# The first loads in smaller parts in order of need, two projections in halves of the channels, and the last scaling in four equal parts

## The chip, the cores and the metric

The kernel runs on one core of one Trainium2 chip. TensorE (PE) multiplies matrices into PSUM, VectorE (DVE) and ScalarE (ACT) do elementwise work, GpSimd (POOL) a little of it, and the queue of SyncE (SP) issues all transfers between the chip's memory and the on-chip buffers. The metric is the device time of one execution in microseconds (us); lower is better. The instructions of an engine stand in one order in the program, and one that waits holds up those behind it on that engine.

## The reference

Two residual layers on 1024 positions of 1024 channels; each is a token mixer and a feed-forward block, with an RMS norm ahead of each and one at the end. What bears on this change is the very beginning, the norm and input projection of layer 0, and the very end, the final norm:

```python
def rms_norm(x, g):
    y = xf * lax.rsqrt(jnp.mean(xf * xf, axis=-1, keepdims=True) + EPS)
    return y * g

def mixer_ab(h, w_in, conv_w, a_log, dt_bias, norm_g, sc_conv_w, w_out):
    qkv, z, beta_raw, alpha_raw, gate_b, gate_c, sc_in = split_cols(h @ w_in, AB_SPLITS)
    qkv = jax.nn.silu(causal_depthwise_conv(qkv, conv_w))
    ...

    h = x
    for layer in range(DEPTH):
        hn = rms_norm(h, norm_mix_g[layer])
        ...
    return rms_norm(h, norm_final_g)
```

## The kernel before

Everything is kept transposed, channels on the 128 partitions: x is 8 tiles of 128 channels (index `d` or `k`) for each of two halves of the sequence (`half`, 512 positions). A float32 product is made of three matmuls on split operands: a value is split into a rounded high part and a rest, and `mm3` issues high x high (L125), high x low (L126) and low x high (L127). `split` (L99 to L102) makes the parts: a CAST on ACT for the high one, then a subtraction on DVE for the rest. A projection (`proj`, L133) is 8 channel tiles x 3 = 24 matmuls of 128x512 into one PSUM bank. Banks come from three rings: "u" with three (`psu`), "m" with three (`psm`), "g" with two (`psg`).

The norm of layer 0 is put off. `scaled_in` (L1878) multiplies a tile of x by the gain `g` alone: ACT makes `hnh`, DVE the rest `hnl`. The projections run on these, and the factor 1/rms, one per position, is multiplied in afterwards. It is made by `squares` and `piece` (ACT squares a tile into `sq`, of which there are two buffers; DVE adds it to `acc`, L186), by `rms` (16 tiny matmuls on `acc` and `sq`, L198; here called the sums; then `v` on DVE, L201, and a power on POOL, L203), and by `spread` (four transposes, L212), after which ACT copies the result to `rb[half]` (L866). `lead` (L849) then multiplies a finished projection by `rb` on DVE into `xp`, which frees its PSUM bank.

At the start one queue issues the loads in the order of the program: the vector of gains `vec`, x tile 0, weight block 0 (128x1024, `raw`), x tiles 1 to 3, the second weight block, x tiles 4 to 7, and so on. Both `raw` buffers are in use by then, so blocks three and four wait until the splits of the first two are done. A weight block holds 8 slices of 128 columns, one for each channel tile.

While `ordered` is open (L1915 to its `close()`), the instructions of PE, DVE and ACT stand in the order in which the code names them; work from behind it (the convolution's `cacc`, L1023 and L1025, and the one-off `na`, L930) may be set between by the scheduler where its cost rules see room. In that stretch PE does, for half 0: two projections, the sums, half of a third projection, the spread, its other half, a fourth projection; then for half 1 one projection, the sums of half 1 (L198 again), a second projection, its spread. The step function `second` (L1885) puts the operands and squares of half 1 between these on ACT and DVE. Behind that come 32 matmuls on the small block `wba` (L902), whose results DVE scales into `bat` (L905) and PE transposes with L907.

At the very end, `last` in `down` computes the last output tile in two halves of 256 positions. For each, `scaled` (L1951) multiplies all 8 channel tiles by the spread 1/rms on DVE and writes them out; three DVE instructions of 4, 2 and 2 channel tiles, each with its own transfer.

Of the kernel before, what the change touches and what calls it, by code (L numbers as in the profile page):

```python
# [18 lines left out]
P = 128  # L19
T_LEN = 1024  # L20
DM = 1024
KT = DM // P
NH = 2
HT = 512
# [4 lines left out]
KH = KT // 2  # L29
# [21 lines left out]
W_AT = weight_chunks()  # L51
# [3 lines left out]
def hybrid_trunk_kernel(ctx: ExitStack, tc: tile.TileContext, x_t, w_all, w_down, w_ba, vecs, c_f, c_i, c_rope, out):  # L55
    nc = tc.nc
    V, S, G, T = nc.vector, nc.scalar, nc.gpsimd, nc.tensor
    dma = nc.sync.dma_start

    def pool(name, side="left", space=None):  # L60
        kw = {} if space is None else {"space": space}
        if space is None:
            kw["side"] = side
        if space is not DRAM:
            kw["reuse_waits"] = "tile"
        return tc.tile_pool(name=name, bufs=1, **kw)
# [22 lines left out]
    def psg():  # L89
        return ps.tile([P, HT], F32, tag="g", name="psg", bufs=2)  # L90
# [8 lines left out]
    def split(hi, lo, src, eng=V):  # L99

        S.copy(hi, src)  # L101
        eng.tensor_tensor(lo, src, hi.bitcast(F32), op=SUB)  # L102
# [15 lines left out]
    def wk(w, i):  # L118

        return tuple(w[i][:, z, :].rearrange("p (k c) -> p k c", k=KT) for z in range(2))  # L120
# [12 lines left out]
    def proj(w, hn, order=range(KT), o=None, first=True, last=True):  # L133
        o = psu() if o is None else o
        mm3(o, [(w[0][:, k, :], w[1][:, k, :], hk(hn, 0, k), hk(hn, 1, k)) for k in order], first, last)
        return o
# [693 lines left out]
    def mixer_ab(hn, rb, hp, tr, first, second, close):  # L830
# [16 lines left out]
        wqk, wvz = first  # L847
# [9 lines left out]
            return xp  # L857

        early = {}
        os3 = [proj(wk(wqk, 0), hn[0]), proj(wk(wqk, 1), hn[0])]  # L860
        r = tr.rms(0)
        os3.append(proj(wk(wvz, 0), hn[0], range(KH), last=False))
        pb = tr.spread(r)
        proj(wk(wvz, 0), hn[0], range(KH, KT), os3[2], first=False)
        second(0)
        S.copy(rb[0], pb)  # L866
        for which, o in enumerate(os3):
            early[0, which] = lead(o, 0)
        early[0, 3] = proj(wk(wvz, 1), hn[0])
        second(1)  # L870
        early[1, 0] = proj(wk(wqk, 0), hn[1])
        second(2)
# [4 lines left out]
        with ExitStack() as es:  # L877
# [9 lines left out]
            raw = fp.tile([P, KT, 8], F32, name="wba_raw")  # L887
# [982 lines left out]

    mes = ExitStack()
    hp = mes.enter_context(pool("mix"))
    dma(vec, vecs)
    tr.begin(0, x_t[0], (0,))
    hn = [[quarter(), quarter()] for _ in range(NH)]
    rb = [hp.tile([P, HT], F32, name=f"rb{half}") for half in range(NH)]

    def scaled_in(half, d):  # L1878

        x, g = tr.at(half, d), vec[:, R_MIX + d:R_MIX + d + 1]  # L1880
        hi, lo = hk(hn[half], 0, d), hk(hn[half], 1, d)
        S.activation(hi, x, AF.Copy, scale=g)
        V.scalar_tensor_tensor(lo, x, g, hi.bitcast(F32), op0=MULT, op1=SUB)  # L1883
# [10 lines left out]
        else:  # L1894
            S.copy(rb[1], tr.spread(r.pop()))

    def coming(name):

        u, raw = unit(), ring.tile([P, DM], F32, tag="raw", name="raw", bufs=2)
        dma(raw, w_all[W_AT[name]])  # L1900
        return u, raw

    def arrived(u, raw):
        split(u[:, 0, :], u[:, 1, :], raw)
        return u

    def squares(half, ds):
# [3 lines left out]
    E = mybir.EngineType  # L1911
    ordered = ExitStack()
    ordered.enter_context(tc.manual_schedule(engines={E.PE, E.DVE, E.Activation}))
    w0 = coming(("ab", 0))
    tr.load(0, x_t[0], range(1, 4))  # L1915
    w1 = coming(("ab", 4))
    tr.load(0, x_t[0], range(4, KT))
    dma(cf[:, 0:P], c_f[:, 0:P])
    scaled_in(0, 0)
    first = [[arrived(*w0)], []]  # L1920
    for d in range(1, 4):
        scaled_in(0, d)
    first[0].append(arrived(*w1))
    w0, w1 = coming(("ab", 8)), coming(("ab", 12))
    ring.tile([P, 24], F32, name="pad")
    tr.begin(1, x_t[1])
# [23 lines left out]

    def scaled(half, cols, pb):  # L1951

        for a, b in ((0, 4), (4, 6), (6, 8)):
            h = tr.h[half][a // KH][:, a % KH:a % KH + b - a, cols]
            V.tensor_tensor(h, h, pb[:, None, :].to_broadcast([P, b - a, pb.shape[1]]), op=MULT)
            dma(out[half, a:b, :, cols].rearrange("k p t -> p k t"), h)
# [135 lines left out]
```

## Time and profile before

| | |
|---|---|
| Time, median of 3 runs | 2595.95 us (2595.7 to 2596.75) |
| Profiled execution: its own time | 2595.86 us |
| Profiled execution: span of the profile | 2594.1 us |
| PE busy | 2574.8 us, 99% of the span |
| DVE, ACT, POOL busy | 1649.9, 1003.9, 457.7 us (64%, 39%, 18%) |
| First projection matmul starts | 7.38 us into the span |
| Last DVE instruction starts its group of three | 2587.56 us |

The span runs from the first to the last event of the profile; 1.76 us of the execution's own time lie outside it. A row of the timeline gives start, duration, engine, source line, operation, and output<-input; "xN" is N such instructions in a row, merged, so that the gap from one to the next is somewhat less than the duration of a single one. What stands in square brackets is how long the engine sat idle before and what ended that.

### The profile page before, as it was taken

What the parts mean: (1) busy time and instruction counts of PE and PEld (TensorE: products, weight loads), DVE (VectorE), ACT (ScalarE), POOL (GpSimd) and SP (SyncE); (2) the same over time, 40 slices, a digit from 0 to 9 for tenths busy, and PEclk for the clock granted to TensorE, in tenths of its full rate; (3) what the DMA queues carried; (4) which work ended last, traced back from release to release, by engine and by line L of the source; (5) the groups of instructions that cost most, each with busy time, mean ns of one, the idle gap of its engine ahead of it and who ended that gap; (6) DMA issues with size and microseconds to landing.
All of it is one profiled execution on the core that took longest, in us unless ns stands there. A gap on an engine that the chain in (4) does not pass through costs nothing.

```text
span 2594.1 us, 36983 instructions
## 1 busy us (share of the span) xinstructions
PE 2574.8 (99%) x14203; PEld 2153.8 (83%) x14203; DVE 1649.9 (64%) x2784; ACT 1003.9 (39%) x1655; POOL 457.7 (18%) x434
## 2 busy tenths in 40 slices
PE   8999999999999999999999999999999999999998
PEld 6888888888888888888888888888888888888887
DVE  7887776585656565564675557478567565566554
ACT  5432123343333345333454345354444333334442
POOL 1110111333333300010000000000034433331001
PEclk9999999999999999999999999999999999999999
DMA  4434446424555688541222322314652455668853
GB/s 143 139 99 153 122 152 213 153 86 162 189 195 204 205 302 284 190 134 62 82 64 73 92 64 62 99 58 127 221 198 70 171 175 202 203 206 282 285 172 122
DMA packets 239697, 402.95 MB, mean 155 GB/s; under 512 B 30080, under 2 KB 114592, under 8 KB 239392
## 3 DMA queue, kind: packets, MB, share of 16 engines
q1 hardware_dynamic: 239520, 400.59, 46.7%
q8 instruction: 111, 1.82, 0.3%
q14 instruction: 66, 0.54, 0.1%
HBM read 280.36 MB, written 120.14 MB: 154 GB/s over the span
## 4 chain that ended last, share of the span: by engine, by line
PE 80%; DVE 2%; issue 0%; ACT 0%; POOLq 0%; POOL 0%; DVEq 0%; ACTq 0%
PE psu L125 16%; PE psu L127 16%; PE psu L126 16%; PE psg L125 5%; PE psg L127 5%; PE psg L126 5%; PE psm L126 4%; PE psm L127 4%; PE psm L125 4%; PE psm L1724 1%; PE psm L1698 1%; PE psg L1489 1%; PE psm L1713 1%; DVE h L586 1%; PE psm L198 0%
## 5 line engine op out<-in xcount | busy, mean ns | idle before, releaser
L125 PE MATMUL psu<-hnh,w 128*128 128x512 f32 x1328 | 530.5, 399 | 7.4 <-ACT w L101 7.4
L127 PE MATMUL psu<-hnh,w 128*128 128x512 f32 x1328 | 520.0, 392 | 0.0
L126 PE MATMUL psu<-hnl,w 128*128 128x512 f32 x1328 | 519.2, 391 | 0.0
L102 DVE TENSOR_TENSOR w<-raw,w 128x1024 fp32r<-128x1024 f32 (+1 forms) x314 | 374.5, 1194 | 150.5 <-ACT w L101 149.5
L101 ACT CAST w<-raw 128x1024 fp32r<-128x1024 f32 (+1 forms) x314 | 306.0, 976 | 298.8 <-PE psu L127 146.7
L125 PEld LDWEIGHTS psu<-hnh,w 128*128 128x128 f32 x1328 | 250.2, 188 | 57.3 <-ACT w L101 7.4
L127 PEld LDWEIGHTS psu<-hnh,w 128*128 128x128 f32 x1328 | 249.8, 188 | 53.7 <-DVE w L102 0.8
L126 PEld LDWEIGHTS psu<-hnl,w 128*128 128x128 f32 x1328 | 250.4, 189 | 49.5 <-DVE hnl L1883 0.6
L186 POOL TENSOR_TENSOR acc<-acc,sq 128x512 f32<-128x512 f32 x48 | 71.6, 1492 | 496.0 <-ACT sq L182 496.0
L102 DVE TENSOR_TENSOR hidq<-hr,hidq 128x1024 fp32r<-128x1024 f32 x72 | 81.5, 1134 | 72.4 <-ACT hidq L101 72.3
L296 POOL TENSOR_TENSOR ws<-raw 128x512 f32<-128x512 f32 x40 | 54.8, 1371 | 355.0 <-DMA raw<-in_dram 249.9
L125 PE MATMUL psu<-w,hnh 128*128 128x512 f32 (+1 forms) x320 | 113.3, 354 | 0.0
L102 DVE TENSOR_TENSOR w<-ws,w 128x1024 fp32r<-128x1024 f32 x38 | 50.7, 1334 | 97.4 <-ACT w L101 97.3
L127 PE MATMUL psu<-w,hnl 128*128 128x512 f32 (+1 forms) x320 | 111.4, 348 | 0.0
L126 PE MATMUL psu<-w,hnh 128*128 128x512 f32 (+1 forms) x320 | 111.3, 348 | 0.0
L101 ACT CAST hidq<-hr 128x1024 fp32r<-128x1024 f32 x72 | 70.2, 979 | 97.6 <-DMA hr<-ts 56.7
L125 PE MATMUL psm<-hidq,w 128*128 128x512 f32 (+1 forms) x275 | 106.1, 386 | 0.0
L126 PE MATMUL psm<-hidq,w 128*128 128x512 f32 (+1 forms) x275 | 106.0, 385 | 0.0
L127 PE MATMUL psm<-hidq,w 128*128 128x512 f32 (+1 forms) x275 | 106.0, 385 | 0.0
L1527 POOL COPY attn<-ac 32x128 f32<-32x128 f32 x32 | 13.3, 416 | 430.8 <-DVE ac L1493 378.4
L125 PE MATMUL psu<-hidq,w 128*128 128x512 f32 (+1 forms) x220 | 84.7, 385 | 0.0
L126 PE MATMUL psu<-hidq,w 128*128 128x512 f32 (+1 forms) x220 | 84.6, 384 | 0.0
(431 smaller groups left out, 5719.3 us busy)
## 6 DMA issues: line engine op xcount, KB each, us to landing
raw<-in_dram SPq DMA_DIRECT2D x228, 512.0 KB, 3.7
sd<-in_dram SPq DMA_DIRECT2D x44, 512.0 KB, 3.8
hid<-hid SPq DMA_DIRECT2D x88, 256.0 KB, 2.7
sd<-sd SPq DMA_DIRECT2D x44, 512.0 KB, 3.3
hr<-ts SPq DMA_DIRECT2D x40, 512.0 KB, 4.2
raw<-sd SPq DMA_DIRECT2D x40, 512.0 KB, 4.4
hd<-h SPq DMA_DIRECT2D x48, 256.0 KB, 3.9
h<-hd SPq DMA_DIRECT2D x48, 256.0 KB, 5.8
```

Of the source, the lines that this page charges most:

```text
L101: S.copy(hi, src)
L102: eng.tensor_tensor(lo, src, hi.bitcast(F32), op=SUB)
L125: T.matmul(o, lh, rh, start=first and i == 0, stop=False, **kw)
L126: T.matmul(o, lh, rl, start=False, stop=False, **kw)
L127: T.matmul(o, ll, rh, start=False, stop=last and i == n - 1, **kw)
L186: (eng or G).tensor_tensor(a, a, q, op=ADD)
L296: G.tensor_tensor(s[:, HT:], b[:, :HT], b[:, HT:], op=ADD)
L586: eng.tensor_tensor(dst, x, y, op=SUB)
L1489: T.matmul(od[r * 32:(r + 1) * 32, c * 32:(c + 1) * 32], a[:, z], x[:, z], start=True, stop=True, tile_position=(0, r * 32))
L1698: T.matmul(o[:, z], self.q[:, j * P:(j + 1) * P], self.k[:, (j - m + 1) * P:(j + 1) * P], start=True, stop=True)
L1713: T.transpose(o[:, i:i + P], s[:, i:i + P], ident)
L1724: T.matmul(po[:, jj * P:(jj + 1) * P], pt[:, z.start + i * P:z.start + (i + 1) * P], self.vp[:, j - m + 1 + i, :], start=i == 0, stop=i == ...
```

## The change

Four things change. (1) `vec` is loaded behind x tile 0 and not ahead of it. Weight block 0 is loaded and split in two parts, the first 2 of its 8 slices and then the other 6, and block 1 as 4 and 4 slices; x tile 1 is loaded and scaled between the parts of block 0. (2) The first two projections are done in four pieces: channels 0 to 3 of the first, 0 to 3 of the second, 4 to 7 of the first, 4 to 7 of the second. (3) The third projection is done whole ahead of the sums of half 0, and it is the fourth that is split by the spread; the fourth gets a bank of the ring "g", the others stay in "u". (4) `scaled` has four instructions of two channel tiles each, and four transfers.

```diff
         early = {}
-        os3 = [proj(wk(wqk, 0), hn[0]), proj(wk(wqk, 1), hn[0])]
+        os3 = [proj(wk(wqk, i), hn[0], range(KH), last=False) for i in range(2)]
+        for i in range(2):
+            proj(wk(wqk, i), hn[0], range(KH, KT), os3[i], first=False)
+        os3.append(proj(wk(wvz, 0), hn[0]))
         r = tr.rms(0)
-        os3.append(proj(wk(wvz, 0), hn[0], range(KH), last=False))
+        early[0, 3] = proj(wk(wvz, 1), hn[0], range(KH), psg(), last=False)
         pb = tr.spread(r)
-        proj(wk(wvz, 0), hn[0], range(KH, KT), os3[2], first=False)
+        proj(wk(wvz, 1), hn[0], range(KH, KT), early[0, 3], first=False)
         second(0)
         S.copy(rb[0], pb)
         for which, o in enumerate(os3):
             early[0, which] = lead(o, 0)
-        early[0, 3] = proj(wk(wvz, 1), hn[0])
         second(1)
         early[1, 0] = proj(wk(wqk, 0), hn[1])
...
+    tr.begin(0, x_t[0], (0,))
     dma(vec, vecs)
-    tr.begin(0, x_t[0], (0,))
...
-    def coming(name):
+    def coming(name, at=DM):
 
         u, raw = unit(), ring.tile([P, DM], F32, tag="raw", name="raw", bufs=2)
-        dma(raw, w_all[W_AT[name]])
-        return u, raw
-
-    def arrived(u, raw):
-        split(u[:, 0, :], u[:, 1, :], raw)
+        dma(raw[:, :at], w_all[W_AT[name]][:, :at])
+        return u, raw, lambda: dma(raw[:, at:], w_all[W_AT[name]][:, at:])
+
+    def arrived(u, raw, _, a=0, b=DM):
+        split(u[:, 0, a:b], u[:, 1, a:b], raw[:, a:b])
         return u
...
-    w0 = coming(("ab", 0))
-    tr.load(0, x_t[0], range(1, 4))
-    w1 = coming(("ab", 4))
+    w0 = coming(("ab", 0), 2 * P)
+    tr.load(0, x_t[0], (1,))
+    w0[2]()
+    tr.load(0, x_t[0], (2, 3))
+    w1 = coming(("ab", 4), HT)
+    w1[2]()
     tr.load(0, x_t[0], range(4, KT))
     dma(cf[:, 0:P], c_f[:, 0:P])
     scaled_in(0, 0)
-    first = [[arrived(*w0)], []]
-    for d in range(1, 4):
+    arrived(*w0, 0, 2 * P)
+    scaled_in(0, 1)
+    first = [[arrived(*w0, 2 * P, DM)], []]
+    for d in range(2, 4):
         scaled_in(0, d)
-    first[0].append(arrived(*w1))
+    arrived(*w1, 0, HT)
+    first[0].append(arrived(*w1, HT, DM))
...
-        for a, b in ((0, 4), (4, 6), (6, 8)):
+        for a in range(0, KT, 2):
+            b = a + 2
```

The rows below are the program's order on one engine; "xN" stands for N like rows in a row, and in brackets is what an instruction waits for. DMAHW0, DMAHW1 and so on are the transfers of SP's queue counted in turn, so that at the start DMAHW0 is the first and DMAHW1 the second; `hnh` and `hnl` are the parts of scaled x, `w` a weight block's parts, `h_97` and `h_96` the x tiles 0 to 3 of half 0. First ACT at the start of the program, before:

```order
L930 ACT_TABLE_LOAD
L930 ACTIVATE na<-vec 128x4 [waits DMAHW0_49]
L1882 ACTIVATE hnh<-h_97,vec 128x512 [waits DMAHW1_49]
L101 CAST w<-raw 128x1024 [waits DMAHW2_49]
L1882 ACTIVATE hnh<-h_97,vec 128x512 [waits DMAHW3_49]
```

The same place with the change:

```order
L1884 ACT_TABLE_LOAD [waits DMAHW1_49]
L1884 ACTIVATE hnh<-h_96,vec 128x512 [waits DMAHW0_49]
L101 CAST w<-raw 128x256 [waits DMAHW2_49]
L1884 ACTIVATE hnh<-h_96,vec 128x512 [waits DMAHW3_49]
L101 CAST w<-raw 128x768 [waits DMAHW4_49]
L1884 ACTIVATE hnh<-h_96,vec 128x512 [waits DMAHW5_49]
```

The loading of the activation table was free of waits and stood ahead of `na`; now it waits for the second transfer, which is `vec`, and `na` has moved behind the first part of block 1.

The second place is DVE between `v` of half 0 and the last of the six additions to `acc` for half 1, `h_145` and `h_146` (with the change `h_151` and `h_152`) being the x tiles of half 1. Before, from `v` to the fourth of the additions:

```order
L201 TENSOR_SCALAR v_262<-psm 128x4
L1883 SCALAR_TENSOR_TENSOR hnl<-h_145,vec,hnh 128x512 x4
L856 TENSOR_TENSOR xp<-psu,rb_108 128x512 x2
L1023 TENSOR_SCALAR cacc<-xp,vec 128x512 x2
L1025 SCALAR_TENSOR_TENSOR cacc<-xp,vec,cacc 128x512
L856 TENSOR_TENSOR xp<-psu,rb_108 128x512
L1883 SCALAR_TENSOR_TENSOR hnl<-h_146,vec,hnh 128x512 x4
L186 TENSOR_TENSOR acc<-acc,sq 128x512
L102 TENSOR_TENSOR wba<-wba_raw,wba 128x8x8
L186 TENSOR_TENSOR acc<-acc,sq 128x512
L1025 SCALAR_TENSOR_TENSOR cacc<-xp,vec,cacc 128x512
L186 TENSOR_TENSOR acc<-acc,sq 128x512
```

With the change:

```order
L201 TENSOR_SCALAR v_293<-psm 128x4
L1885 SCALAR_TENSOR_TENSOR hnl<-h_151,vec,hnh 128x512 x4
L102 TENSOR_TENSOR wba<-wba_raw,wba 128x8x8
L856 TENSOR_TENSOR xp<-psu,rb_108 128x512 x3
L1885 SCALAR_TENSOR_TENSOR hnl<-h_152,vec,hnh 128x512 x4
L186 TENSOR_TENSOR acc<-acc,sq 128x512
L1025 TENSOR_SCALAR cacc<-xp,vec 128x512
L186 TENSOR_TENSOR acc<-acc,sq 128x512
L1027 SCALAR_TENSOR_TENSOR cacc<-xp,vec,cacc 128x512
L186 TENSOR_TENSOR acc<-acc,sq 128x512
```

In both, the operands of half 1 and all additions for half 1 stand behind `v`, but `v` waits for the sums of half 0, and on PE these have moved back by one projection: 72 matmuls stand ahead of them where 48 did. From the sums of half 0 to those of half 1 PE has 48 projection matmuls and the spread where it had 72 and the spread. After the rows shown, the rest with the change runs: `cacc`, addition, `cacc`, addition, `cacc` (L1025), addition; among the six additions stand five instructions on `cacc`, two of L1025 and three of L1027. Two more orders change further on: four projection matmuls and not nine stand between the last matmul on `wba` and the first L907 (L909 with the change), and on DVE one of two weight splits that stood ahead of the two `xp` of half 1 has moved behind `bat`.

## The prediction

> **What bounds the kernel now.** I read the page's busy times first, then PE's waits, then the timeline around the two ends and around each place where an instruction has moved.
>
> ```profile
> PE 2574.8 (99%) x14203; PEld 2153.8 (83%) x14203; DVE 1649.9 (64%) x2784; ACT 1003.9 (39%) x1655; POOL 457.7 (18%) x434
> ```
>
> PE is busy for 2574.8 of 2594.1 us. Whatever keeps it from starting, idles it or prolongs the tail comes out one for one; nothing later can take it back.
>
> ```profile
> PE psu L125 <- ACT w L101: 7.4, 1, 7.4
> ```
>
> Of PE's waits this one is by far the longest: 7.4 us in total, once, for the cast of the first weight block.
>
> **The start.**
>
> ```profile
> 0.73 1.28 ACT L930 ACT_TABLE_LOAD   x1 [0.73 <-PEq L2081]
> ...
> 0.73 0.39 SPq L1873 DMA_DIRECT2D vec<-in_dram  x1
> ...
> 1.19 0.41 SPq L166 DMA_DIRECT2D h<-in_dram  x1
> ...
> 2.65 0.20 ACT L930 ACTIVATE na<-vec 128x4 f32<-128x4 f32 x1 [0.64 <-DMA vec<-in_dram]
> ...
> 4.50 0.72 ACT L1882 ACTIVATE hnh<-h,vec 128x512 fp32r<-128x512 f32 x1 [1.64 <-DMA h<-in_dram]
> ...
> 6.29 1.04 ACT L101 CAST w<-raw 128x1024 fp32r<-128x1024 f32 x1 [1.07 <-DMA raw<-in_dram]
> ...
> 7.38 0.80 PE L125 MATMUL psu<-hnh,w 128*128 128x512 f32 x1 [7.38 <-ACT w L101]
> ...
> 10.09 0.63 PE L127 MATMUL psu<-hnh,w 128*128 128x512 f32 x1
> ...
> 10.50 2.56 ACT L1882 ACTIVATE hnh<-h,vec 128x512 fp32r<-128x512 f32 x4
> 10.52 0.63 PE L125 MATMUL psu<-hnh,w 128*128 128x512 f32 x1
> ...
> 11.25 0.40 PE L127 MATMUL psu<-hnh,w 128*128 128x512 f32 x1
> ...
> 13.15 0.40 PE L125 MATMUL psu<-hnh,w 128*128 128x512 f32 x1
> ...
> 13.38 0.40 PE L126 MATMUL psu<-hnl,w 128*128 128x512 f32 x1
> ```
>
> Before, the table load costs nothing: it runs from 0.73 to 2.01 while ACT waits for data anyway. Now it waits for `vec`, the second transfer. `vec` took 1.92 us from issue to use (0.73 to 2.65). Issued second, at 1.19, it cannot land before 3.11; and since `vec` and x tile 0 together were in at 4.50, not after 4.50. As its bytes follow x tile 0's in the same queue I take 3.9. Then 1.28 of table load (ACT at 5.2, bounds 4.4 to 5.8), the first `hnh` (0.64, a quarter of 2.56) and the cast of 256 columns (0.4: nearest is 1.04 for 1024) put the first matmul at 6.3, not 7.38.
>
> The first matmuls follow one another at 0.43 us (10.09 to 10.52); from about 11.05, 3.7 us after the first, at 0.23 us (13.15 to 13.38). The row at 13.15 is matmul 15, counted from 0; matmul 24 is thus at 13.15 + 9 x 0.23 = 15.2. With the change, if the pace picks up 3.7 us after the start, 8.6 matmuls are out by 10.0 and number 24 comes at 10.0 + 15.4 x 0.23 = 13.5; if at 11.05 as before, 11 are out and it comes at 14.0; if only at 13.7, at 15.3. The operands allow about this pace: ACT reaches x tile 4 at 5.2 + 4 x 0.64 + 2 x 1.04 for the casts' columns + 0.4 for `na` and the start-up of two more casts = 10.2, against 10.50 before; two more splits cost DVE some 0.2 each. SP issues two more transfers ahead of x tile 4, 0.46 each (0.73 to 1.19), but the same bytes stand ahead of it as before and ACT wants it no sooner. Gain 1.1 us, bounds 1.7 and -0.1.
>
> **The sums of half 1: a new wait.**
>
> ```profile
> 21.02 1.05 PE L198 MATMUL psm<-onesn,acc 128*128 128x1 f32 x8 [0.17 <-DVE acc L186]
> ...
> 23.01 0.16 DVE L201 TENSOR_SCALAR v<-psm 128x4 f32<-128x4 f32 x1 [1.90 <-PE psm L198]
> 23.09 2.74 DVE L1883 SCALAR_TENSOR_TENSOR hnl<-h,vec,hnh 128x512 fp32r<-128x512 f32 x4
> ...
> 25.67 0.60 PE L212 MATMUL psm<-cf,r 128*128 128x128 f32 x4
> ...
> 26.92 1.29 DVE L856 TENSOR_TENSOR xp<-psu,rb 128x512 f32<-128x512 f32 x2 [1.09 <-ACT rb L866]
> ...
> 28.12 0.88 DVE L1023 TENSOR_SCALAR cacc<-xp,vec 128x512 f32<-128x512 f32 x2
> ...
> 28.91 0.74 DVE L1025 SCALAR_TENSOR_TENSOR cacc<-xp,vec,cacc 128x512 f32<-128x512 f32 x1
> ...
> 29.58 0.68 DVE L856 TENSOR_TENSOR xp<-psu,rb 128x512 f32<-128x512 f32 x1
> ...
> 30.18 2.73 DVE L1883 SCALAR_TENSOR_TENSOR hnl<-h,vec,hnh 128x512 fp32r<-128x512 f32 x4
> ...
> 32.82 0.69 DVE L186 TENSOR_TENSOR acc<-acc,sq 128x512 f32<-128x512 f32 x1
> ...
> 34.83 0.69 DVE L186 TENSOR_TENSOR acc<-acc,sq 128x512 f32<-128x512 f32 x1
> ...
> 35.43 0.75 DVE L1025 SCALAR_TENSOR_TENSOR cacc<-xp,vec,cacc 128x512 f32<-128x512 f32 x1
> ...
> 38.56 0.68 DVE L186 TENSOR_TENSOR acc<-acc,sq 128x512 f32<-128x512 f32 x1
> ...
> 39.73 0.95 PE L198 MATMUL psm<-onesn,acc 128*128 128x1 f32 x8
> ```
>
> At the sums of half 0 PE waited 0.17 us for the additions on DVE. Now a third projection stands ahead of them, and that wait and its restart go: 0.3 gained.
>
> Count from these sums (21.02 before). Before, PE reaches the sums of half 1 18.7 us later, and the last addition ends at 39.24, 18.2 later: 0.5 to spare. From one start to the next on DVE: `xp` 0.60 (29.58 to 30.18), four `hnl` 2.65, addition 0.60 (34.83 to 35.43), L1025 0.67 (28.91 to 29.58), L1023 0.40. Now PE has one projection (24 x 0.23 = 5.5) fewer in between and arrives 18.7 - 5.5 = 13.2 us after the sums of half 0. DVE's work is still tied to them: `v`, then the spread 4.65 after the sums (21.02 to 25.67), the first `xp` 1.25 behind it, at 5.90; three `xp` 1.8, four `hnl` 2.65: first addition at 10.35. Up to the sixth it takes five additions 3.0, two L1023 0.8 and three L1027 (the old L1025) 2.0, and the sixth itself 0.69: its end is at 16.85. PE waits 16.9 - 13.2 = 3.7 us. ACT doesn't bound it: its squares for half 1 follow the `hnh` behind `rb`, and with two `sq` buffers each is ready some 0.5 us before its addition. The weight cast between them waits for PE's projection, which ends ahead of this wait. Bounds: 2.6, if DVE has 1.1 us less than I count, and 4.5, if ACT's squares come late.
>
> The other moved edges cost nothing: the three "u" banks are free again when `xp` 1 to 3 are done, 6.5 to 7.7 after the sums, while PE wants the first of them at 7.8; the `hnl` of tiles 4 to 7 are made from 7.7 on, wanted from 10.5.
>
> **Behind it, `bat`.**
>
> ```profile
> 41.61 0.16 DVE L201 TENSOR_SCALAR v<-psm 128x4 f32<-128x4 f32 x1 [1.30 <-PE psm L198]
> ...
> 48.30 1.23 DVE L102 TENSOR_TENSOR w<-raw,w 128x1024 fp32r<-128x1024 f32 x1
> ...
> 55.41 0.67 DVE L905 TENSOR_TENSOR bat<-psu,rb 16x512 f32<-16x512 f32 x1
> ...
> 56.97 1.05 PE L907 MATMUL psm<-cf,bat 16*128 16x8 f32 x8
> ```
>
> `bat` is ready at 56.08, 0.9 before L907 uses it. Now L907 stands five matmuls earlier (1.1 us), and between `v` and the `xp` DVE has one L1023 and two L1025 more (1.7) and one weight split less (1.2), so `bat` comes 0.5 later: 1.1 + 0.5 - 0.9 = 0.7 us of wait (0 to 1.5). The weight split behind `bat` is for the projection after the next, 4 us off.
>
> **The end.**
>
> ```profile
> 2587.56 2.42 DVE L1955 TENSOR_TENSOR h<-h,psm 128x1024 f32<-128x1024 f32 x3 [1.37 <-PE psm L212]
> 2588.81 1.70 SPq L1956 DMA_DIRECT2D out_dram<-h  x3
> ```
>
> The first transfer waits for the first instruction, some 1.15 us of the 2.42. With two tiles it takes about 0.65 and the transfer goes out 0.5 earlier.
>
> ```profile
> 2584.00:2585.00 1.00, 0.28 (x3) 0.20 (x2) 1.00 (x3) 0.15 (x1) 0.00 (x0) 1.00 0.22 79
> ...
> 2588.00:2589.00 1.00, 0.00 (x0) 0.00 (x0) 1.00 (x2) 0.00 (x0) 0.00 (x0) 0.59 0.00 0
> ...
> 2590.00:2591.00 1.00, 0.00 (x0) 0.00 (x0) 0.00 (x0) 0.00 (x0) 0.00 (x0) 0.50 1.08 384
> ```
>
> A row is a stretch with the busy times of PE, PEld, DVE, ACT and POOL, PE's granted clock, the share of the transfer engines and GB/s. While the last megabyte is written, the transfer engines are full (share 1.08, 384 GB/s), so what starts sooner ends sooner: gain 0.4. If the last piece's latency decided instead, a fourth instruction's start-up would cost 0.2. The first 256 positions have time; the addition on DVE behind three of their four pieces is some 0.1 later, which I set off here.
>
> **Sum.** Against the profiled execution: -1.1 (start) - 0.3 (first sums) + 3.7 (sums of half 1) + 0.7 (`bat`) - 0.4 (end) = +2.6, and 2595.86 + 2.6 = 2598.5 us. Its 2595.86 is 0.09 under the median, which changes nothing.
>
> **Rivals.** (a) Faster: the additions of half 1 are in time, so that PE doesn't wait. This needs DVE 3.7 us sooner, the sixth addition ended 13.2 after the sums. For it: DVE would be idle for some 5 us ahead of `v`. Against: all of it stands behind `v`. Then `bat` is in time too, and -1.1 - 0.3 - 0.4 = -1.8: 2594.1.
>
> (b) The wait slows PE's clock. PE ran dry in 2584 to 2585 (0.28 busy), and the granted clock was at 1.00 then, at 0.59 in 2588 to 2589 and at 0.50 later, so some 4 us of little work on PE halve it. A wait of 3.7 us is just short of that. If it falls, the 24 matmuls behind run at 0.43 for up to the 3.7 us of the start, 8.6 matmuls at 0.20 more each: +1.7, 2600.2. [...]
>
> (c) The change doesn't do what it says at the start: the table load behind `vec` eats the time won, or the pace picks up late. Gain 0 in place of 1.1: 2599.6. For it: the wait on the table load's row in the order; against: the first block's part is there 1 to 2 us sooner. [...]
>
> ```profile
> 1297.88 1.28 ACT L1446 ACT_TABLE_LOAD   x1
> 1299.18 0.60 ACT L1446 ACTIVATE q<-psu 128x512 f32<-128x512 f32 x1
> ```
>
> Here the next instruction starts 0.02 behind a table load, so I add none. [...]
>
> **Chances.** My sum 52%, (a) 9%, (b) 20%, (c) 16%, other 3%. Rivals (b) and (c) together reach 2601.3. The range is 2595.6 to 2601.2: it leaves out (a) and the upper parts of (b) and of other waits; my own case is 2597 to 2600. A difference of 0.2%, 5.2 us, is about what a measurement of this kernel can tell from no change. Faster than 2590.8 nothing here can give (3% for what I overlook); slower than 2601.1 needs (b) with (c) or a longer wait: 14%; within: 83%.
>
> **What would show it.** Right: the table load starting after 3 us, the first matmul near 6.3, PE's list of waits with L198 on DVE `acc` for 3 to 4 us near 39 to 42 us, one below 1 us on `bat`, and the last transfer issued in four pieces from 2588.3 on, shifted by the sum. Wrong: no wait of PE ahead of the second L198; matmuls at 0.43 behind it (rival b); a first matmul after 7 us (rival c); or a difference that lies behind 65 us, where the order is unchanged.

## The result

The changed kernel takes 2602.09 us (median of 17 runs, 2599.45 to 2604.33), the kernel before, run beside it, 2596.35 (17 runs, 2595.70 to 2598.68): a ratio of 1.0021, 95% interval 1.0013 to 1.0028. It is 5.7 us slower, some 0.2%. I had forecast 2598.5 with a range up to 2601.2, so the time lies 0.9 us beyond it. The profiled execution of the changed kernel took 2601.01 us, its span is 2599.2, 5.1 longer than before.

PE's list of waits in the changed kernel, the four longest of the beginning (in total, times, longest, in us):

```profile
PE psu L125 <- ACT w L101: 6.0, 1, 6.0
PE psm L198 <- DVE acc L186: 3.4, 1, 3.4
PE psu L126 <- DVE hnl L1885: 0.5, 1, 0.5
PE psu L125 <- ACT hnh L1884: 0.4, 1, 0.4
```

The first weight block is waited for 6.0 us and not 7.4; new is the wait of 3.4 us of the sums (L198) for DVE's additions. Nothing waits for `bat`. The timeline of the changed kernel at the start, from the sums of half 0 to the spread of half 1, and at the end:

```profile
3.68 1.28 ACT L1884 ACT_TABLE_LOAD   x1 [3.68 <-DMA vec<-in_dram]
4.97 0.72 ACT L1884 ACTIVATE hnh<-h,vec 128x512 fp32r<-128x512 f32 x1
6.04 0.79 PE L125 MATMUL psu<-hnh,w 128*128 128x512 f32 x1 [6.04 <-ACT w L101]
...
10.43 0.50 PE L126 MATMUL psu<-hnl,w 128*128 128x512 f32 x1 [0.53 <-DVE hnl L1885]
...
14.46 0.39 PE L125 MATMUL psu<-hnh,w 128*128 128x512 f32 x1
...
25.34 0.95 PE L198 MATMUL psm<-onesn,acc 128*128 128x1 f32 x8
...
31.16 1.89 DVE L856 TENSOR_TENSOR xp<-psu,rb 128x512 f32<-128x512 f32 x3 [0.99 <-ACT rb L869]
...
41.40 0.68 DVE L186 TENSOR_TENSOR acc<-acc,sq 128x512 f32<-128x512 f32 x1
...
42.13 1.05 PE L198 MATMUL psm<-onesn,acc 128*128 128x1 f32 x8 [3.44 <-DVE acc L186]
...
44.47 0.77 PE L125 MATMUL psu<-hnh,w 128*128 128x512 f32 x1
...
49.31 0.63 PE L127 MATMUL psu<-hnh,w 128*128 128x512 f32 x1
49.73 0.61 PE L125 MATMUL psu<-hnh,w 128*128 128x512 f32 x1
...
52.73 0.60 PE L212 MATMUL psm<-cf,r 128*128 128x128 f32 x4
...
2593.34 2.48 DVE L1964 TENSOR_TENSOR h<-h,psm 128x512 f32<-128x512 f32 x4 [1.32 <-PE psm L212]
2594.05 2.16 SPq L1965 DMA_DIRECT2D out_dram<-h  x4
```

The row at 14.46 is matmul 24, which was at 15.24. From 44.47 on the matmuls follow one another at 0.43 us (49.31 to 49.73), which is also the pace of this profile's first matmuls (7.55 to 7.98); in the kernel before they ran at 0.23 here (45.43 to 45.66). The granted clock (the column after the five busy times) in slices of one microsecond of the changed kernel:

```profile
40.00:41.00 1.00, 0.00 (x0) 0.00 (x0) 1.00 (x2) 1.00 (x3) 0.38 (x1) 1.00 0.00 0
...
42.00:43.00 1.00, 0.86 (x8) 0.87 (x8) 0.68 (x2) 0.00 (x0) 0.00 (x0) 1.00 0.00 0
43.00:44.00 1.00, 1.00 (x8) 1.00 (x8) 0.00 (x0) 0.00 (x0) 0.00 (x0) 0.69 0.00 0
44.00:45.00 1.00, 1.00 (x4) 0.95 (x5) 0.36 (x2) 0.00 (x0) 0.11 (x1) 0.50 0.00 0
...
49.00:50.00 1.00, 1.00 (x4) 0.81 (x3) 1.00 (x3) 0.63 (x1) 0.00 (x0) 0.50 0.00 0
50.00:51.00 1.00, 1.00 (x5) 0.76 (x5) 1.00 (x3) 0.59 (x1) 0.49 (x1) 0.90 0.00 0
```

In the kernel before, a slice of the projection behind the sums of half 1 (39.73 to 41.44) has the clock at 1.00:

```profile
44.00:45.00 1.00, 1.00 (x7) 0.81 (x6) 1.00 (x3) 0.42 (x1) 0.00 (x0) 1.00 0.00 0
```

DVE works through 40 to 41 us while PE has nothing; at about 43.4 PE's clock falls to half and comes back at 50.2 (a slice of 0.69 is 62% of it at half, one of 0.90 is 20%). So the 5.1 us of the two spans come from these places, each a difference of times between the same two rows in both kernels:

| Stretch | Before | After | Difference |
|---|---|---|---|
| span's start to matmul 24 | 15.24 | 14.46 | -0.78 |
| matmul 24 to the sums of half 0, less the added projection (24 x 0.227 = 5.45) | 5.78 | 5.43 | -0.35 |
| sums of half 0 to sums of half 1, less that projection in the kernel before | 13.26 | 16.79 | +3.53 |
| sums of half 1 to the next projection | 1.71 | 2.34 | +0.63 |
| that projection, to the spread of half 1 | 5.58 | 8.26 | +2.68 |
| spread of half 1 to the last scaling on DVE (2587.56, 2593.34) | 2540.54 | 2540.61 | +0.07 |
| last scaling to the end of the span | 6.54 | 5.86 | -0.68 |

The sum is +5.1. The wait is one half of the loss, 3.5 us; the low clock behind it, 0.63 + 2.68 = 3.3 us, is the other. The table compares one execution of each kernel; its first row differs from execution to execution, as the section on the prediction shows.

### The profile page after: what moved, and what is told of

The parts are those of the page before. It is cut to its first block, busy times and chain, and to the rows that moved or that the text cites. A ratio compares the mean times of both kernels' runs of the same rounds, so it can differ in the third digit from the quotient of the medians.

```text
span 2599.2 us, 36995 instructions
## 1 busy us (share of the span) xinstructions
PE 2577.7 (99%) x14203; PEld 2154.5 (83%) x14203; DVE 1651.6 (64%) x2788; ACT 1003.9 (39%) x1657; POOL 460.2 (18%) x434
## 4 chain that ended last, share of the span: by engine, by line
PE 80%; DVE 2%; issue 0%; ACT 0%; POOLq 0%; POOL 0%; DVEq 0%; ACTq 0%
PE psu L125 16%; PE psu L127 16%; PE psu L126 16%; PE psg L125 5%; PE psg L126 5%; PE psg L127 5%; PE psm L125 4%; PE psm L127 4%; PE psm L126 4%; PE psm L1726 1%; PE psm L1700 1%; PE psg L1491 1%; PE psm L1715 1%; DVE h L586 1%; PE psm L198 0%
## 5 line engine op out<-in xcount | busy, mean ns | idle before, releaser
L102 DVE TENSOR_TENSOR w<-raw,w 128x1024 fp32r<-128x1024 f32 (+2 forms) x316 | 375.2, 1189 | 149.2 <-ACT w L101 147.7
L101 ACT CAST w<-raw 128x1024 fp32r<-128x1024 f32 (+2 forms) x316 | 306.2, 970 | 302.2 <-PE psu L127 144.6
```

## The experiments

My theory after the result: DVE's additions for half 1 come too late because they stand behind `v`, which waits for sums that moved back by a projection; this wait costs its own 3.5 us and another 3.3 by the clock. Rivals: that the low clock has nothing to do with the wait, that the loss lies in the start or in the transfers, or that each of the parts is slower by itself.

### The wait filled with matmuls

The changed kernel with 15 matmuls of 128x512 ahead of the sums of half 1, whose result is not read; nothing else differs.

```diff
         elif step == 2:
+            o, w, b = psm(), wk(first[0], 1), hn[1]
+            for k in range(15):
+                T.matmul(o, w[0][:, k % KT, :], hk(b, 0, k % KT), start=True, stop=True)
             r.append(tr.rms(1))
```

> The changed kernel with 15 extra matmuls of 128x512, whose result nothing reads, between the first projection of half 1 and the sums of half 1: they fill most of the 3.4 us in which PE waits there for DVE's additions. Theory (two costs: the wait itself, and the clock that falls because PE idles): the sums still start near 42.1 us, as the additions set it, but the granted clock stays at 1.00 and the 24 matmuls behind follow at 0.23 us; some 3.3 us less than the changed kernel, so about 2.4 us over the kernel before. Rival (the slow matmuls after 43 us have another cause, such as their operands or transfers): matmuls at 0.43 us there all the same, time as the changed kernel's, 5.5 to 6 us over before.

Measured: 2599.07 us (11 runs; ratio to the kernel before 1.0009, 1.0000 to 1.0018). The sums come at nearly the same time (41.81 and 42.13), since DVE ends no sooner, but the median is 3.0 us below that of the changed kernel, which is nearly all of the 3.3. In its profile, however, the clock fell all the same, later and for a shorter time. Its timeline around the sums of half 1:

```profile
38.12 3.56 PE L1897 MATMUL psm<-hnh,w 128*128 128x512 f32 x15
...
41.81 1.02 PE L198 MATMUL psm<-onesn,acc 128*128 128x1 f32 x8
42.70 1.03 PE L198 MATMUL psm<-onesn,sq 128*128 128x1 f32 x8
...
50.77 0.60 PE L212 MATMUL psm<-cf,r 128*128 128x128 f32 x4
```

And its slices of one microsecond, with the granted clock behind the five busy times:

```profile
44.00:45.00 1.00, 1.00 (x5) 0.77 (x4) 1.00 (x3) 0.00 (x0) 0.99 (x1) 0.65 0.00 0
45.00:46.00 1.00, 1.00 (x4) 0.81 (x3) 1.00 (x2) 0.00 (x0) 0.46 (x1) 0.50 0.00 0
...
47.00:48.00 1.00, 1.00 (x4) 0.83 (x3) 1.00 (x2) 0.63 (x1) 0.58 (x1) 0.64 0.00 0
```

PE's list of waits has none here; nearly all that could count as little work are the 16 matmuls of one column, 1.8 us. (The last 128x512 matmul ahead of them and the first behind them start 2.30 us apart, where 1.93 is usual, so some 0.4 us are lost as well.) The half clock lasts from 44.3 to 47.7. The same kernel ran once more:

> The changed kernel with 15 unread matmuls in the place of the wait, once more. In the first profile the clock fell for about 3 us behind the sums of half 1 though PE was not idle, only on 16 matmuls of 128x1 for 1.8 us. If stretches with so little work can be enough, depending on where they fall in the clock's period, the fall comes again in some executions and not in others, 3.4 us long; if the clock stays at 1.00 from 40 to 52 us, the first was an exception and the spread of half 1 comes about 1.7 us sooner behind the sums (7.2 instead of 9 us).

The second execution took 2597.52 us, and its clock stayed at 1.00, as two of its slices show:

```profile
44.00:45.00 1.00, 1.00 (x7) 0.87 (x7) 0.67 (x2) 0.00 (x0) 0.43 (x1) 1.00 0.00 0
45.00:46.00 1.00, 1.00 (x6) 0.83 (x5) 1.00 (x3) 0.00 (x0) 1.00 (x1) 1.00 0.00 0
```

The spread comes 7.32 us behind the sums (42.38 to 49.70), against 8.96 in the first and 10.60 in the changed kernel. So with PE kept at work the clock fell in one of two profiles, with nearly the same gap between the 128x512 matmuls (2.30 and 2.31 us); without that it fell in every profile with such a wait. The counts further below tell these two profiles apart.

### The operands and sums of half 1 made early

The changed kernel, but all eight tiles of half 1 are scaled ahead of the sums of half 0 on ACT and DVE, and its squares and additions stand right behind `v`, ahead of the three `xp`.

```diff
+        second(0)
         r = tr.rms(0)
+        second(1)
         early[0, 3] = proj(wk(wvz, 1), hn[0], range(KH), psg(), last=False)
         pb = tr.spread(r)
         proj(wk(wvz, 1), hn[0], range(KH, KT), early[0, 3], first=False)
-        second(0)
         S.copy(rb[0], pb)
         for which, o in enumerate(os3):
             early[0, which] = lead(o, 0)
-        second(1)
...
-        if step < 2:
-            for d in range(KH * step, KH * step + KH):
+        if step == 0:
+            for d in range(KT):
                 scaled_in(1, d)
-            if step:
-                squares(1, range(KT))
+        elif step == 1:
+            squares(1, range(KT))
```

> The changed kernel with the operands of half 1 (all eight tiles) ahead of the sums of half 0 on ACT and DVE, and its squares and additions right behind them, ahead of the copy of rb and the three xp. Theory: the additions end some 10 us after the sums of half 0 in place of 16.8, PE waits nowhere before the sums of half 1, the clock stays up; 6.5 us less than the changed kernel, 0.7 to 1.7 us under the kernel before (start -0.7, first sums -0.3, end -0.7, up to 0.7 lost on bat). Rival (the wait is bound by something else than the place of these instructions, ACT's squares for one): PE still waits more than 1 us on acc or sq, time 1 to 6 us over before.

Measured: 2594.13 us (11 runs; ratio to the kernel before 0.9990, 0.9982 to 0.9999), 8 us less than the changed kernel and 0.1% less than the kernel before, with an interval that ends just under 1. Its timeline, from the sums of half 0 to those of half 1:

```profile
27.63 0.95 PE L198 MATMUL psm<-onesn,acc 128*128 128x1 f32 x8
...
29.59 0.68 DVE L186 TENSOR_TENSOR acc<-acc,sq 128x512 f32<-128x512 f32 x1
...
30.51 3.87 DVE L186 TENSOR_TENSOR acc<-acc,sq 128x512 f32<-128x512 f32 x5
...
41.07 0.95 PE L198 MATMUL psm<-onesn,acc 128*128 128x1 f32 x8
```

And its slice with the second sums:

```profile
41.00:42.00 1.00, 1.00 (x12) 0.96 (x10) 0.41 (x1) 1.00 (x2) 0.64 (x2) 1.00 0.00 0
```

The sixth addition ends at 34.4, some 6.7 us before PE wants it; the two sums are 13.4 us apart, which is PE's own work (13.2 by the prediction), and the clock stays up. The order of DVE's work was the cause of both halves of the loss. This is the case without a wait that rival (a) described. That its 2594.1 is also the median here is in part luck: in the profiled execution, of 2595.86 us, matmul 24 came at 16.73, 1.5 us later than in the kernel before, where (a) has it 1.1 earlier.

### Each part alone

The kernel before with part (3) alone, the third projection ahead of the sums:

```diff
         os3 = [proj(wk(wqk, 0), hn[0]), proj(wk(wqk, 1), hn[0])]
+        os3.append(proj(wk(wvz, 0), hn[0]))
         r = tr.rms(0)
-        os3.append(proj(wk(wvz, 0), hn[0], range(KH), last=False))
+        early[0, 3] = proj(wk(wvz, 1), hn[0], range(KH), psg(), last=False)
         pb = tr.spread(r)
-        proj(wk(wvz, 0), hn[0], range(KH, KT), os3[2], first=False)
+        proj(wk(wvz, 1), hn[0], range(KH, KT), early[0, 3], first=False)
...
-        early[0, 3] = proj(wk(wvz, 1), hn[0])
```

> The kernel before with part (3) alone: the third projection whole ahead of the sums of half 0, the fourth split by the spread, in a bank of ring g. Theory: this part alone makes the wait: 3.4 to 3.7 us on acc before the sums of half 1 and then half the clock; without the start's and the end's gain that is 6 to 7 us over the kernel before (3 us where the clock happens to hold). Rival (the wait comes from the smaller loads and splits at the start, which set DVE back): no wait there, time within 0.5 us of before.

Measured: 2603.93 us (8 runs; ratio 1.0026, 1.0016 to 1.0036). The sums of half 1 in its timeline:

```profile
43.41 1.86 PE L198 MATMUL psm<-onesn,acc 128*128 128x1 f32 x8 [3.45 <-DVE acc L186]
```

And the slices in which its clock falls and comes back:

```profile
42.00:43.00 1.00, 0.00 (x0) 0.00 (x0) 1.00 (x3) 1.00 (x2) 0.41 (x1) 0.59 0.00 0
...
51.00:52.00 1.00, 1.00 (x4) 0.81 (x3) 1.00 (x2) 0.42 (x1) 0.00 (x0) 0.50 0.00 0
52.00:53.00 1.00, 1.00 (x5) 0.77 (x5) 1.00 (x3) 0.43 (x2) 0.12 (x1) 0.79 0.00 0
```

The same wait to 0.01 us, and here the clock falls before the wait is over and stays down for 10.2 us. Part (3) alone brings the whole loss.

The kernel before with parts (1) and (2), so with the changed loads and the first two projections in halves of the channels, but the third projection split by the spread as before:

```diff
         for i in range(2):
             proj(wk(wqk, i), hn[0], range(KH, KT), os3[i], first=False)
-        os3.append(proj(wk(wvz, 0), hn[0]))
         r = tr.rms(0)
-        early[0, 3] = proj(wk(wvz, 1), hn[0], range(KH), psg(), last=False)
+        os3.append(proj(wk(wvz, 0), hn[0], range(KH), last=False))
         pb = tr.spread(r)
-        proj(wk(wvz, 1), hn[0], range(KH, KT), early[0, 3], first=False)
+        proj(wk(wvz, 0), hn[0], range(KH, KT), os3[2], first=False)
...
+        early[0, 3] = proj(wk(wvz, 1), hn[0])
```

> The kernel before with parts (1) and (2) alone: smaller loads and the first two projections in halves, but projections three and four, the sums and the last scaling as before. Theory: the first matmul at 6.0 and the 25th 0.7 us earlier, but the additions for half 0 end at 21.7 as in the changed kernel (before 20.97), so the gain is lost in a wait of some 1.8 us at the sums of half 0, which start near 21.75, 0.7 later than before: 0.5 to 1 us over the kernel before. Rival (the start's gain is kept): 0.7 to 1 us under the kernel before.

Measured: 2598.13 us (11 runs; ratio 1.0004, 0.9995 to 1.0013): no difference that can be told. PE is earlier by the 0.8 us, but the additions of half 0 are not, as its timeline shows at the sums of half 0:

```profile
21.64 1.05 PE L198 MATMUL psm<-onesn,acc 128*128 128x1 f32 x8 [1.59 <-DVE acc L186]
```

Its slices behind that:

```profile
23.00:24.00 1.00, 1.00 (x7) 1.00 (x7) 0.27 (x2) 0.90 (x2) 0.03 (x1) 0.67 1.02 369
24.00:25.00 1.00, 1.00 (x4) 0.71 (x4) 1.00 (x2) 0.00 (x0) 1.00 (x1) 0.50 0.97 385
...
26.00:27.00 1.00, 1.00 (x5) 0.76 (x4) 0.55 (x1) 0.00 (x0) 0.00 (x0) 0.63 0.12 37
```

The wait at the first sums grows from 0.17 to 1.59 us, and even that lets the clock fall, from 23.3 to 26.7. So part (3) does have a use: it takes the wait from the first sums. Without an earlier place for the operands of half 1 it moves it to the second.

The kernel before with part (4) alone:

```diff
-        for a, b in ((0, 4), (4, 6), (6, 8)):
+        for a in range(0, KT, 2):
+            b = a + 2
```

> The kernel before with part (4) alone: four DVE instructions of two channel tiles and four transfers in the last scaling. By my term for the end it is 0.4 us faster, and by the end gain read from the changed kernel's trace (its last sums are 5.76 us later than before, its span is 5.1 us longer) 0.66 us; a ratio of 0.9997 to 0.9998, which is within what the runs can tell from 1. Up to the last sums the trace should be that of before. If instead the last transfer's latency sets the end and a fourth instruction only adds its start-up, the span from the last sums to the end is 0.2 us longer than before and not shorter.

Measured: 2597.16 us (11 runs; ratio 1.0001, 0.9992 to 1.0010), nothing that the times can show. In its timeline the last scaling starts 5.69 us behind the spread of the first 256 positions (in the kernel before 5.44, from 2582.12 to 2587.56), and the span ends 6.0 us behind it, at 2594.4 (before: 6.54):

```profile
2582.70 0.38 PE L212 MATMUL psm<-cf,r 128*128 128x128 f32 x2
...
2588.39 2.48 DVE L1956 TENSOR_TENSOR h<-h,psm 128x512 f32<-128x512 f32 x4 [1.56 <-PE psm L212]
```

The tail behind the last scaling is 0.5 shorter, some 0.25 is lost ahead of it. That loss is not the part's: the clock fell at 2587.1 here, ahead of the last spread, whose two L212 took 0.69 us, and in the kernel before only at 2588.2, behind it (0.43 us). In the changed kernel the tail is 0.68 shorter and nothing is lost ahead. By the traces the part is worth 0.5 to 0.7 us where the clock falls no earlier.

### The activation table loaded early

The changed kernel, with an activation of one column, whose result is not read, ahead of everything on ACT:

```diff
-    const.tile([P, 8], F32, name="pad")
+    pad = const.tile([P, 8], F32, name="pad")
     V.memset(mhalf, -0.5)
+    S.activation(pad[:, 0:1], mhalf[:, 0:1], AF.Exp)
```

> The changed kernel with one more activation of one column ahead of everything on ACT, which needs no loaded data, so that the activation table is loaded before `vec` lands and not behind it. If the table load behind `vec` (3.68 to 4.97 us in the changed kernel) is what keeps the first `hnh` from starting, `hnh` starts near 3.7 instead of 4.97 and the first matmul near 4.8 to 5.1 instead of 6.04; the time then falls by 0.6 to 1.3 us, depending on when the pace of the first matmuls doubles. The wait at the sums of half 1 and the low clock behind it stay. If x tile 0 or the first part of the weight block is what is late, the first matmul stays at 5.7 to 6.1 and the time with it.

Measured: 2602.28 us (11 runs; ratio 1.0021, 1.0013 to 1.0030), the same as the changed kernel. Its timeline of ACT at the start:

```profile
0.73 1.28 ACT L88 ACT_TABLE_LOAD   x1 [0.73 <-PEq L2091]
2.02 0.20 ACT L88 ACTIVATE pad<-mhalf 128x1 f32<-128x1 f32 x1
3.86 0.72 ACT L1885 ACTIVATE hnh<-h,vec 128x512 fp32r<-128x512 f32 x1 [1.63 <-DMA vec<-in_dram]
5.92 0.40 ACT L102 CAST w<-raw 128x256 fp32r<-128x256 f32 x1 [1.34 <-DMA raw<-in_dram]
```

The first `hnh` starts 1.1 us sooner as expected, but then ACT waits 1.34 us for the first part of the weight block, and the first matmul starts at 6.37. In this execution the table load behind `vec` would have cost nothing, since what it would have been late for was later still. With the operands of half 1 made early as well:

> The operands, squares and additions of half 1 moved ahead of the sums of half 0 (as in the run that did that alone) and the early table load together. If both causes are right and independent: no wait of PE at the sums of half 1, granted clock at 1.00 there, first matmul near 5; the time 0.6 to 1.3 us below that of the run with the moved operands (2594.1), so 2592.8 to 2593.5, about 3 us below the kernel before and 8 to 9 below the changed one. If the earlier start brings PE to the operands of half 0 sooner than ACT and DVE can make them, waits of 0.3 to 1 us appear among the first 48 matmuls and the time stays at 2594.

Measured: 2595.42 us (11 runs; ratio 0.9992, 0.9983 to 1.0001), not faster than with the moved operands alone. In this profile the first part of the block was there in time and the first matmul started at 5.14, yet matmul 24 came at 16.84, since some of the first ones came 0.2 to 0.6 us late for their operands and the pace doubled only at matmul 20. In the profile of the kernel with the operands moved it doubled nearly as late, at matmul 18, with matmul 24 at 16.73; in the changed kernel's at matmul 7, with 14.46.

### PE at work from the start

The changed kernel with 11 matmuls of 128x512 on a constant tile ahead of the first projection, whose result is not read:

```diff
+    wt = unit()
+    V.memset(wt[:, 0, :P + HT].bitcast(F32), 1.0)
+    o = psm()
+    for k in range(11):
+        T.matmul(o, wt[:, 0, :P], wt[:, 0, P:P + HT], start=True, stop=True)
     w0 = coming(("ab", 0), 2 * P)
```

> The changed kernel with 11 matmuls of 128x512 on a constant tile ahead of the first projection, whose result nobody reads; they run while PE would wait for the first loads. If the low pace of the first matmuls (0.43 us for one until 10.4 to 14 us into the span) is PE's clock that has not come up yet, the 11 take about 4.7 us at that pace, end before the first operands are there, and the projection's first matmuls follow at 0.23 from the start or soon behind it; then ACT's operands set the pace, tile 4 being there at about 11.1 us, so the 25th matmul comes at 11.5 to 12.5 instead of 14.46 and the time falls by 2 to 3 us, to 2599 to 2600. The wait at the sums of half 1 stays, or grows by up to 1 us where the additions of half 0 become late. If the low pace comes from late operands, or the 11 matmuls end behind 6 us, nothing is gained.

Measured: 2601.96 us (11 runs; ratio 1.0018, 1.0009 to 1.0027): nothing gained. Its timeline at the start:

```profile
1.65 5.06 PE L1920 MATMUL psm<-w 128*128 128x512 f32 x11 [1.65 <-DVE w L1917]
...
10.00 0.50 PE L126 MATMUL psu<-hnl,w 128*128 128x512 f32 x1 [0.54 <-DVE hnl L1885]
...
14.38 0.39 PE L125 MATMUL psu<-hnh,w 128*128 128x512 f32 x1
```

The pace does double at the second matmul, at 7 us (0.43 us from 6.50 to 6.93, 0.23 from 7.26 to 7.49), so I take the low pace of the first matmuls for a clock that has not come up: 0.43 us is also what one takes at a granted clock of 0.50, as from 49.31 to 49.73 in the changed kernel. But then PE waits for the operands of x tiles 1 to 3 until 10.0, and matmul 24 comes at 14.38, where it was at 14.46. With these loads a clock that is up from the start doesn't bring matmul 24 ahead of some 14 us: it came at 14.26 and 14.23 in the next two kernels, and at 14.0 to 14.6 without the 11 matmuls wherever the pace doubled at matmul 7. My 11.1 for x tile 4 had left the waits before it out. The 11 matmuls on the kernel with the operands of half 1 made early, and on that one with the early table:

> The kernel with the operands and sums of half 1 moved ahead of the sums of half 0, with the same 11 matmuls at the start. Both causes together: no wait and a clock of 1.00 at the sums of half 1, and a start 2 to 3 us sooner; 2594.1 less 2 to 3, so 2591 to 2592, and the runs no longer in two groups 2 us apart if these come from the moment at which the pace doubles. If DVE, which now has all operands of half 1 ahead, becomes the bound, a wait of 1 to 3 us appears at the sums of half 0 or 1 and the time stays at 2593 to 2595.

> As the run before with the activation table loaded early as well. The early table load alone brought nothing, since the pace of the matmuls doubled later by as much. With PE running already, the first projection matmul at 5 to 5.2 instead of 6.0 to 6.3 should tell: 0.5 to 1 us less than the run before it, 2590 to 2591.5; if the 11 matmuls end behind 5.2 us, or the first operands wait for their transfers, it is the same as that run.

Measured: 2594.06 us (11 runs; ratio 0.9990, 0.9981 to 0.9999) and 2594.08 (11 runs; ratio 0.9988, 0.9979 to 0.9997). Both are faster than the changed kernel and, by 0.1%, than the kernel before, and both take as long as the one with the operands moved alone (2594.13), the simplest of the three. That the 11 matmuls save only those executions in which the pace doubles late would fit 9 of 11 runs below 2595 where 6 of 11 were without them, but this is too few runs to show it.

### The changed kernel again

> The changed kernel once more, to see whether the fall of the clock behind the wait at the sums of half 1 repeats, and how long it lasts. If the clock is judged in stretches of about 3.4 us and falls when one of them is nearly empty, the wait of 3.4 us makes it fall in most executions and the half clock lasts one or two such stretches, 3.4 or 6.8 us, so that the spread of half 1 starts 27.4 us behind the sums of half 0 (as in the first profile, 25.34 to 52.73) or some 1.7 us sooner; without a fall it would come some 3 us sooner.

It took 2601.41 us: wait 3.44 us, sums of half 0 at 25.38, and the clock down from 43.6 to 50.4. Over all profiles of the study in which PE waited more than 1 us at the sums, the fall came every time, and its length, worked out from the mixed slices at its ends, is a multiple of 3.4 us. The last column is explained below the table.

| Kernel | Wait at the sums | Half clock | Length | 128x512 matmuls started: in the step ahead; in each step at half clock |
|---|---|---|---|---|
| parts (1) and (2) alone | 1.59 | 23.3 to 26.7 | 3.4 | 0; 8 |
| early table | 3.44 | 46.0 to 49.4 | 3.4 | 0; 7 |
| changed | 3.44 | 43.4 to 50.2 | 6.8 | 0; 6, 8 |
| changed, again | 3.44 | 43.6 to 50.4 | 6.8 | 0; 6, 8 |
| part (3) alone | 3.45 | 42.2 to 52.4 | 10.2 | 4; 0, 5, 8 |
| PE at work from the start | 3.53 | 41.3 to 51.5 | 10.2 | 2; 0, 6, 8 |

Each 3.4 us at half pace holds 8.0 matmuls of 0.43 us, each 0.2 us slower, so by this estimate it costs 1.6, and less where part of it lies in the wait itself. Which of the three lengths comes does not go by the wait, which is nearly the same in the last five.

The traces show what it goes with. In each profile all changes of the clock lie on a grid with steps of 3.413 us, whose place differs from profile to profile: in the changed kernel the clock comes up at 9.24, falls at 43.37 and comes back at 50.20, which is 34.13 us, or ten steps, and then 6.83, or two. In the kernel before it comes up at 11.11 and falls at 2588.17, 755 steps (of 3.4133) later. For each step of the first 70 us I counted the matmuls of 128x512 that start in it, in all 14 profiles. At full clock, at most 15 or 16 fit: behind each of the 7 steps with five or fewer the clock was at half, behind each of the 216 with six or more it stayed at full. At half clock, 8 fit: it stayed at half behind every step with five or fewer and came up behind every one with seven or eight; with six, five steps left it down and two brought it up; the steps ahead of the first rise, at a pace of 0.43 us, are among these. The one-column matmuls are not in these counts. So in these profiles the fall and its length go with where the grid cuts the stretch of little work; that these counts are the cause was not shown. This also tells the two profiles with the wait filled apart: the step with most of the sums had five matmuls of 128x512 in the first, and seven in the second.

## Why the prediction was wrong

- **The start**, -1.1: right in sign, measured -0.78, within the bounds. The first matmul came at 6.04 where I had 6.3, and the table load at 3.68 where I had 3.9. What held matmul 24 back was waits for the operands of x tiles 1 to 3 (0.4 and 0.5 us in the list), which I had set at nothing; the run with PE at work from the start shows that with the clock up they alone keep it at 14.4. But the size is partly luck. In three of the eight profiles with the changed loads and no matmuls ahead the clock came up only at 15.3 to 15.9 us, and matmul 24 at 16.7 to 16.8, outside my bounds; with the old loads it came at 15.24, 15.73 and 16.17. The waits bear on this, too: in these three profiles two steps in a row held only five or six matmuls. So the late pace of rival (c) does occur, though not in the profiled execution of the changed kernel; loading the table early brought nothing more.
- **The first sums**, -0.3: measured -0.35.
- **The sums of half 1**, +3.7: the wait is 3.44 and the stretch 3.53 us longer. Counting DVE's instructions behind `v` against PE's matmuls gave the size to 0.3 us, and the run with the operands moved shows that this order was the cause.
- **`bat`**, +0.7: measured 0. It ended at 61.20 for L909 at 61.54. PE had been put back by 3.3 us of low clock in the meantime, DVE, whose `xp` wait for the spread, by only 1.9 (`bat` comes 18.4 us behind the sums, and 16.5 in the profile with the wait filled whose clock stayed up). Whether 0.7 would come without the fall stays open: in no run did PE wait for it, but in that profile eleven projection matmuls and not four stood ahead of L909.
- **The end**, -0.4: measured -0.68 in the changed kernel, -0.3 with the part alone, -0.5 without what its earlier fall of the clock took.
- **The clock**, rival (b), which I gave 20% and +1.7: this is the step that failed, twice. First in the choice: I set the wait of 3.7 us against "some 4 us of little work on PE" and called it just short. But the sums behind the wait are 16 matmuls of one column, 1.7 us in which PE starts no full matmul either (39.73 to 41.44 in the kernel before). The stretch of little work was 3.44 + 1.7 = 5.1 us, well over those 4; and the tail's own row, with its 0.28 of PE busy on such sums, belonged to what I compared with. By the counts above, 3.7 + 1.7 = 5.4 us without such work leave some step at least 2.7 of its 3.4 us empty, with room for three or four matmuls, so by this estimate the fall had to come wherever the grid lay, and not with 20%. Second in the price: I let the half clock last no longer than 3.7 us as at the start; it lasted 6.8, the first step at half clock holding part of the sums and only six matmuls, a count that left it down behind five of seven steps, and it slowed the sums too, 3.3 us in place of 1.7. With both right the sum is 2598.5 + 3.3 = 2601.8, and the errors of the other terms (`bat` -0.7, end -0.3, wait -0.2, start +0.3) make it 2600.9; the profiled execution took 2601.01.

Nor does a fall take a wait of 3.4 us: 1.59 us of idle time next to such sums was enough with parts (1) and (2) alone (half clock from 23.3 to 26.7), and so was a step that still held five matmuls in the first profile with the wait filled (44.3 to 47.7).

## What to carry to other kernels

When work moves on the engine that bounds the kernel, follow also what is tied to its results on other engines: here a projection moved ahead of the sums of half 0 put back all that stands behind them on DVE, and the remedy was to take out of that line what didn't need the sums. Price a wait of PE with what stands next to it: in this kernel a wait of 1.59 us and the tiny matmuls beside it, 3.9 us from one full matmul to the next, brought the clock down, and each 3.4 us of half clock that followed a wait cost up to 1.6 us more, so that by this estimate the true cost of a 3.4-us wait was 5 to 8 us. In these profiles the start-to-start gap between the full matmuls on either side told the risk: at the sums 1.93 us left the clock up in all 19 cases, 2.3 to 2.4 us brought it down in one of three, 3.9 us and more in all six. A start that was made earlier paid only as far as the next operand was there: with the 11 matmuls ahead, matmul 24 came at 14.38 and not at 14.46.

## What was not expected of the hardware

The clock fell after a wait of only 1.59 us ahead of the sums, and once, of two profiles of the same kernel, with no wait in PE's list at all, behind 1.8 us of one-column matmuls; in all other profiles the sums without a wait left it at 1.00. Which it was went, in the 14 profiles, with the count of 128x512 matmuls in one step of the grid of 3.413 us: at full clock five or fewer stood ahead of all seven falls and six or more in the 216 steps without one; at half clock it came up behind every step with seven or eight, behind two of seven with six and behind none with fewer. The length of the fall came in whole steps, 3.4, 6.8 and 10.2 us, for nearly equal waits (3.44 to 3.53). At the start the slices show a granted clock of 1.00 while the matmuls run at 0.43 (10:11 in the kernel before): the clock's records begin only where the pace doubles (11.11 us in the kernel before, 9.24 in the changed one), so ahead of that I went by the pace and not by this column. And the moment at which it came up varied: in the profiles with the changed loads and no matmuls ahead it was matmul 7 in five, with matmul 24 at 14.0 to 14.6 us, and matmul 17 to 20 in three, with 16.7 to 16.8.
